# Merge weights of a head pair right behind its last scores: moving the merge of dilated attention forward by two groups

## The chip, the cores and the metric

The kernel runs on one core of one Trainium2 chip. The metric is the device time of one execution in microseconds. The engines are called PE (matmuls; PEld are its weight loads), DVE, ACT, POOL and SP as in the profile. The instructions of each stand in one queue in a fixed order; DMAs are issued from such queues too, here from SP and POOL.

## The reference

One layer of a decoder: RMSNorm, one projection, two mixers side by side, output projection, a conv FFN. The change touches mixer A for the prompt of 2048 positions, softmax attention of 8 heads of 64 elements over three patterns:

```python
PATTERNS = ((128, 1), (512, 4), (2048, 16))      # window, dilation

def combine_patterns(results):
    outs = jnp.stack([o for o, _ in results], axis=0)
    lses = jnp.stack([l for _, l in results], axis=0)
    w = jax.nn.softmax(lses, axis=0)
    return jnp.sum(w[..., None] * outs, axis=0)

def prompt_attn(q, k, v):
    return combine_patterns([dilated_prompt(q, k, v, w, d) for w, d in PATTERNS])
```

Each pattern gives an output and the logarithm of its softmax denominator; the three outputs are merged per head and position with weights from the three denominators.

## The kernel before

The program has three stages: the projections with the linear-attention mixer and the sample tokens (`sweeps`), the prompt's dilated attention (`attention`), and the output projection and FFN (`tail`). A planner sets the order of instructions on each engine: it goes by the order in which they are written, by its own estimate of when each is ready, and by order edges (`after`) that the program adds by hand.

`attention` goes through 4 pairs of heads (`pr`), in each through 3 patterns (`pat`), in each through 4 groups of query blocks (`g`): 12 groups to a pair. A group is one unit (pattern 2) or two (patterns 0 and 1). A unit (`AtUnit`) has three steps. `qk_` does its scores on PE (L1817), their masking and row minimum on DVE (L1822), and the exponentials with their row sums on ACT (L1826); minima and sums go to the statistics tile `aml` of the pair and pattern. `t` transposes the exponentials on PE (L1843) and copies them out of PSUM (L61 on ACT or L63 on DVE). `pv` multiplies by the values (L1860), and the last unit of a group copies the result (L63) into `OP[pat]`, the tile `aop`. Units wait in a list, `fifo`: `drain(3)` lets up to three units be behind in their `pv`. PE's unit steps are chained by hand in the order written.

Patterns 1 and 2 read their queries in an order that needs a gather: POOL copies them into `aqg` (`at_gather`, L1125, two copies to a group), called from `qk_` two groups ahead, in the groups 2 to 9 of each pair, for the groups 4 to 11.

`at_merge` merges the three outputs of one pair. It is a generator: each `next` issues one step. For the pairs 0 to 2:

- step 1, the weights: 8 selecting matmuls bring the statistics of patterns 0 and 2 into one order (`pam`, L1134 and L1137), then a chain of small DVE instructions (L1143 to L1175) with one exponential on ACT (L1166), a transpose on PE (L1189) and a copy to `awt` (L63);
- step 2: POOL stores `awt` to memory (`d_awd`, L1194);
- step 3: POOL issues the loads that bring the weights of the first block of columns back, each spread over 64 partitions (`awb`, L1182);
- then two steps for each of four blocks of columns: (a) the loads of the next block, two products and an addition (L1224, L1224, L1209), and (b) a product, an addition into `amo` and the store to `mixa` (L1224, L1234, L1236), all on POOL.

`line` chains all of these POOL instructions and the gathers in the order in which they are written, so POOL's queue is the program's order. At the end of every group `attention` issues one step of the merge that is under way. Before the change a merge was created when the pair's last unit left `fifo`, which is in the second group of the next pair; so step 1 stood at the end of group 1 of the next pair, the store at the end of group 2, the first loads at the end of group 3, and the blocks in groups 4 to 11. The `aop` pool has 5 tiles, `awb` 2, `amo` 2, `aqg` 5.

The last pair (`pr` 3) does without memory: POOL does the small steps of its weights, POOL and ACT spread them (L1219, L1217), PE transposes them (`pab`, L1221) and DVE multiplies (L1222). All of it is written behind the last unit's values.

Of the kernel before, what the change touches and what calls it, by code (L numbers as in the profile page):

```python
# [36 lines left out]
class Layer:  # L37
# [944 lines left out]
    def attention(self):  # L982
        with ExitStack() as ctx:
            self.aq[1] = self.pool(ctx, "at1")
            p = self.ap = self.pool(ctx, "at")
            self.app = self.pool(ctx, "atp", bass.MemoryType.PSUM)
            self.ev = 0
            pend = None
            fifo = []
            sk = self.AB["skew"]  # L990

            def drain(n):
                nonlocal pend
                if len(fifo) > sk[0]:
                    fifo[-1 - sk[0]].t()
                while len(fifo) > n:
                    un = fifo.pop(0)
                    un.t()
                    un.pv()
                    if un.last:  # L1000
                        for _ in pend or ():
                            pass
                        pend = self.at_merge(un.pr, un.ML, un.OP)

            if self.AB['man']:
                eng = mybir.EngineType
                ctx.enter_context(self.tc.manual_schedule(engines={getattr(eng, e) for e in self.AB['man']}))
            self.vq = []
            self.at_loadv(0)
            self.at_loadv(1)  # L1010
            for _ in self.at_load(0, ((1, 2),), to=self.qk0):
                pass
            rest = self.at_load(0, ((2, 4),), to=self.qk0)
            self.qgn = []
            for _ in range(self.AB["qg"]):
                p.tile([128, 4, 128], F32R, name=self.n("aqg"), tag="aqg", bufs=self.AB["qg"])
            for pat in range(3):
                for _ in range(2):
                    p.tile([128, 16, 4], F32, name=self.n("aml"), tag=f"aml{pat}", bufs=2)
            for _ in range(2):  # L1020
                p.tile([128, 3, 4, 128], F32, name=self.n("awb"), tag="awb", bufs=2)
            for _ in range(2):
                p.tile([128, 512], F32, name=self.n("amo"), tag="amo", bufs=2)
            pre = iter(())
            for pr in range(4):
                if pr == 3:
                    self.rctx.close()
                    pre = self.wo_pre()
                qk = self.qk0
                nxt = self.at_load(pr + 1) if pr < 3 else iter(())  # L1030
                ML, OP = [], []
                for pat in range(3):
                    base = 16 * (3 * pr + pat)
                    ml = p.tile([128, 16, 4], F32, name=self.n("aml"), tag=f"aml{pat}", bufs=2)
                    op = p.tile([128, 4, 512], F32, name=self.n("aop"), tag="aop", bufs=self.AB["op"])
                    ML.append(ml)
                    OP.append(op)
                    for g in range(4):
                        if base // 4 + g + 2 < 48:
                            self.at_loadv(base // 4 + g + 2)  # L1040
                        for _ in rest:
                            pass
                        po = [None]
                        nu = 1 if pat == 2 else 2
                        for u in range(nu):
                            fifo.append(AtUnit(self, pr, pat, g, u, nu, qk, base, ML, OP, po))
                            fifo[-1].qk_()
                            drain(sk[1])
                            if pat:
                                next(pre, None)  # L1050
                        if pend is not None:
                            next(pend, None)
                        if 5 <= 4 * pat + g < 11:
                            self.qk0 = next(nxt, self.qk0)
            for _ in pre:
                pass
            drain(0)
            for _ in pend:
                pass
# [53 lines left out]
    def line(self, ins):  # L1113

        if self.atpo is not None:
            self.after(ins, self.atpo)
        self.atpo = ins
        return ins
# [10 lines left out]
    def at_merge(self, pr, ML, OP):  # L1129
# [48 lines left out]
        def weights(cb):  # L1178
            W = p.tile([128, 3, 4, 128], F32, name=self.n("awb"), tag="awb", bufs=2)
            if not last:  # L1180
                for h in range(2):
                    line(nc.gpsimd.dma_start(W[64 * h:64 * h + 64],  # L1182
                                           bass.AP(tensor=wd.tensor, offset=wd.offset + 1536 * (2 * cb + h),
                                                   ap=[[0, 64], [512, 3], [128, 4], [1, 128]])))
            return W

        if not last:
            pt = pp.tile([128, 512], F32, name=self.n("pab"), tag="am", bufs=AB["am"])
            nc.tensor.transpose(pt[:96, :128], awf, self.ident)  # L1189
            wt = p.tile([128, 512], F32, name=self.n("awt"), tag="amo", bufs=2)[:96, :128]  # L1190
            self.evac(wt, pt[:96, :128], "v")
            wd = self.a["awd"][pr]
            yield
            line(nc.gpsimd.dma_start(wd, wt))  # L1194
            yield
            nxt = weights(0)
            for _ in range(AB["mw"]):
                yield
        tags = ("am", "ao", "ao")
        j = 0  # L1200
        for cb in range(4):
# [811 lines left out]
```

## Time and profile before

| | |
|---|---|
| time, median of 3 runs | 2808.04 us (2801.09 to 2809.57) |
| profiled execution: time, span, granted clock | 2800.35 us, 2798.5 us, 0.98 |
| PE, DVE, ACT, POOL busy | 2682.2, 1841.5, 1269.1, 593.4 us |
| DMA | 656.82 MB, mean 235 GB/s |
| first and last scores of prompt attention (L1817) | 776.8 and 1073.8 us |

A line of the profile gives the engine, the line of the kernel, the operation, the tile written and those read (numbers left out), and its form. In the order of time it begins with the start and the busy time in us and may end with the idle time of that engine ahead of it and what ended it, in brackets. A line of waits gives the waiting engine, tile and line, what it waited for, the sum in us, the number of waits and the longest. A line of stretches gives each engine's busy time with the number of its instructions, the granted clock of TensorE (1.00 is full speed), the share of DMA and GB/s.

### The profile page before, as it was taken

The numbers are of one execution on the slowest core, as the hardware profiler recorded it, in microseconds if no ns is written. First come the engines' busy times: TensorE is split into PE (matmuls) and PEld (weight loads), VectorE is DVE, ScalarE is ACT, GpSimd is POOL, SyncE is SP. The second block draws the span as 40 slices with busy tenths as digits, with TensorE's granted clock in tenths as the row PEclk, the third lists the DMA queues.
The fourth block names the chain that finished last, engine by engine and source line by source line (L and its number), as shares of the span: only waits on it lengthen the run. The fifth ranks groups of instructions, "written<-read, shape, count | busy, mean of one in ns | idle before, by whom it ended". The sixth has DMA issues, their size and how long they took to land. (4 is left out here: it accounts for less than half of the span.)

```text
span 2798.5 us, 58530 instructions
## 1 busy us (share of the span) xinstructions
PE 2682.2 (96%) x22203; PEld 2538.9 (91%) x22203; DVE 1841.5 (66%) x4578; ACT 1269.1 (45%) x2959; POOL 593.4 (21%) x741
## 2 busy tenths in 40 slices
PE   7999999999989998998999998999999999999997
PEld 6889899788778887998899998999999999999997
DVE  7667655444357777466999888676577766666666
ACT  6535433333257776344554444434244333343332
POOL 3424242443333666013000011000020000200001
PEclk9999999999999999998999999999999999999998
DMA  8755446789798764367578677886698875976654
GB/s 302 258 177 181 168 129 208 269 329 361 269 211 174 185 165 141 102 231 254 195 275 297 224 273 291 290 297 223 211 333 282 298 237 198 328 255 215 219 186 147
DMA packets 283594, 656.82 MB, mean 235 GB/s; under 512 B 31841, under 2 KB 81633, under 8 KB 281265
## 3 DMA queue, kind: packets, MB, share of 16 engines
q1 hardware_dynamic: 253008, 574.66, 61.1%
q0 software_dynamic: 13216, 46.56, 5.1%
q10 hardware_dynamic: 17088, 31.86, 3.1%
q8 instruction: 175, 2.87, 0.4%
q14 instruction: 107, 0.87, 0.1%
HBM read 509.02 MB, written 143.94 MB: 233 GB/s over the span
## 5 line engine op out<-in xcount | busy, mean ns | idle before, releaser
L68 ACT ACTIVATE ws<-wr 128x512 fp32r<-128x512 f32 (+1 forms) x482 | 292.9, 616 | 432.4 <-PE pfe L1585 139.1
L90 PE MATMUL pfd<-hh,ws 128*128 128x264 f32 x2816 | 476.9, 286 | 8.3 <-ACT ws L68 6.7
L90 PEld LDWEIGHTS pfd<-hh,ws 128*128 128x128 f32 x2816 | 401.4, 189 | 11.2 <-ACT ws L68 8.6
L71 DVE TENSOR_TENSOR ws<-wr,ws 128x512 fp32r<-128x512 f32 (+1 forms) x482 | 320.0, 670 | 135.8 <-ACT ws L68 131.0
L90 PE MATMUL pfd<-hl,ws 128*128 128x264 f32 x1408 | 303.7, 285 | 0.0
L1585 PE MATMUL pfa<-xh,ws 128*128 128x264 f32 x1496 | 292.8, 287 | 6.8 <-ACT ws L68 2.4
L1585 PE MATMUL pfe<-xh,ws 128*128 128x264 f32 x1496 | 288.6, 285 | 4.2 <-DVE u L1572 2.9
L1585 PE MATMUL pfd<-xh,ws 128*128 128x264 f32 x1408 | 288.0, 285 | 2.8 <-DVE up L1572 2.4
L1585 PEld LDWEIGHTS pfa<-xh,ws 128*128 128x128 f32 x1496 | 237.3, 190 | 8.7 <-ACT p L1574 2.9
L1585 PEld LDWEIGHTS pfe<-xh,ws 128*128 128x128 f32 x1496 | 235.9, 189 | 4.9 <-DVE u L1572 3.3
L398 PE MATMUL pv<-wh,xh 128*128 128x256 f32 (+1 forms) x816 | 234.1, 287 | 1.1 <-DVE th L695 1.1
L1585 PEld LDWEIGHTS pfd<-xh,ws 128*128 128x128 f32 x1408 | 230.7, 189 | 3.8 <-DVE up L1572 3.0
L398 PE MATMUL pv<-wl,xh 128*128 128x256 f32 (+1 forms) x816 | 232.0, 284 | 0.0
L398 PE MATMUL pv<-wh,xl 128*128 128x256 f32 (+1 forms) x816 | 231.9, 284 | 0.0
L90 PEld LDWEIGHTS pfd<-hl,ws 128*128 128x128 f32 x1408 | 226.8, 189 | 0.1
L1534 POOL DMA_DIRECT2D xl<-d_xst x52 | 28.6, 550 | 894.5 <-PE pfe L1585 866.0
L1826 ACT ACTIVATE ass<-ass,aml 128x256 f32<-128x256 f32 (+1 forms) x384 | 173.6, 454 | 89.8 <-DVE aml L1822 88.6
L1585 PE MATMUL pfd<-xl,ws 128*128 128x264 f32 x704 | 200.2, 285 | 0.0
L90 PE MATMUL pq<-xh,wh 128*128 128x512 f32 (+2 forms) x480 | 175.4, 373 | 10.2 <-ACT xh L236 7.7
L1613 DVE TENSOR_TENSOR acc<-acc,pfd 128x264 f32<-128x264 f32 x304 | 116.7, 424 | 91.0 <-PE pfd L90 90.9
L1585 PE MATMUL pfe<-xl,ws 128*128 128x264 f32 x616 | 175.4, 285 | 0.0
L1585 PE MATMUL pfa<-xl,ws 128*128 128x264 f32 x616 | 175.2, 284 | 0.0
(341 smaller groups left out, 6691.4 us busy)
## 6 DMA issues: line engine op xcount, KB each, us to landing
ws<-d_wst SPq DMA_DIRECT2D x248, 512.0 KB
wr<-in_wu SPq DMA_DIRECT2D x114, 512.0 KB
d_wst<-ws SPq DMA_DIRECT2D x88, 512.0 KB
wr<-in_wd SPq DMA_DIRECT2D x160, 256.0 KB
wr<-in_wt SPq DMA_DIRECT2D x60, 512.0 KB
wh<-d_wbs SPq DMA_DIRECT2D x35, 512.0 KB
wl<-d_wbs SPq DMA_DIRECT2D x35, 512.0 KB
skp<-in_ckt SPq DMA_DIRECT2D x16, 1024.0 KB
```

What stands on the lines that cost most here:

```text
L68: h = nc.scalar.activation(hi, src, AF.Copy)
L71: return h, (nc.gpsimd if lo_eng == "p" else nc.vector).tensor_tensor(lo, src, hi.bitcast(F32), op=ALU.subtract)
L90: mm = nc.tensor.matmul(o, ww[:, k, :], xx[:, s0:s0 + n], start=(k == order[0] and i == 0), stop=(k == order[-1] and i == 2))
L398: mm = nc.tensor.matmul(ps[:m, :256], x[:, t0:t0 + m], w[:, k % 4, :], start=(k == 0 and i == 0), stop=(k == KT - 1 and i == 2))
L1534: self.nc.gpsimd.dma_start(t.bitcast(F32), xo[i, z])
L1585: self.lastmm = nc.tensor.matmul(bank[:, :H], w[:, ww, k, :], xx, start=new and k == 0 and j == 0, stop=k == 3 and j == 2, skip_group_chec ...
L1613: nc.vector.tensor_tensor(acc[m][:, s0:s0 + n], acc[m][:, s0:s0 + n], pz, op=ALU.add)
L1826: ex = nc.scalar.activation(ssb[:, sc:sc + nk], ssb[:, sc:sc + nk], AF.Exp, bias=self.ml[:, idx, h:h + 1], scale=-1.0, accum_out=self.ml[: ...
```

## The change

A merge is created in the group that issues the pair's last scores, as soon as the last unit is in `fifo`, and its first step is issued at the end of that group (group 11 of the pair itself). All steps of the pairs 0 to 2 so stand two groups further ahead: the store at the end of group 0 of the next pair, the first loads at the end of group 1, the blocks in groups 2 to 9. For the last pair a `yield` splits the generator behind the weights: the weights are written in group 11, ahead of the last units' transposes and values, and the rest behind them as before. The generators take 12 steps as before.

```diff
@@ attention, in drain() @@
                     un = fifo.pop(0)
                     un.t()
                     un.pv()
-                    if un.last:
-                        for _ in pend or ():
-                            pass
-                        pend = self.at_merge(un.pr, un.ML, un.OP)
@@ attention, in the loop over groups @@
                             drain(sk[1])
                             if pat:
                                 next(pre, None)
+                        if fifo[-1].last:
+                            for _ in pend or ():
+                                pass
+                            pend = self.at_merge(pr, ML, OP)
                         if pend is not None:
                             next(pend, None)
@@ at_merge @@
             nxt = weights(0)
             for _ in range(AB["mw"]):
                 yield
+        else:
+            yield
         tags = ("am", "ao", "ao")
```

## The prediction

> **What bounds the kernel now.** I read the page first, then the busy time by stretches of the attention stage, then its waits, then the order of time on POOL, PE and DVE around the three merges that are moved.
>
> ```profile
> span 2798.5 us, 58530 instructions
> PE 2682.2 (96%) x22203; PEld 2538.9 (91%) x22203; DVE 1841.5 (66%) x4578; ACT 1269.1 (45%) x2959; POOL 593.4 (21%) x741
> 860.00:880.00 20.00, 19.97 (x209) 17.31 (x208) 17.88 (x81) 17.92 (x65) 2.74 (x3) 1.00 0.99 190
> 920.00:940.00 20.00, 17.22 (x154) 15.63 (x156) 11.89 (x46) 11.67 (x48) 16.86 (x16) 0.83 0.94 212
> 980.00:1000.00 20.00, 14.69 (x130) 12.89 (x127) 8.41 (x53) 12.91 (x58) 19.45 (x21) 0.88 0.65 167
> PE pas L1817 <- POOL aqg L1125: 17.1, 9, 4.0
> POOL aop L1224 <- DMA awb<-d_awd: 17.8, 3, 9.4
> ```
>
> PE is busy for 96% of the span, so the kernel as a whole is TensorE's. The three stretches (columns after the length: PE, PEld, DVE, ACT, POOL, granted clock, DMA share, GB/s) show that a pair of prompt attention has two halves. From 860 to 880 PE is full and POOL nearly idle; from 920 to 940 and from 980 to 1000 POOL is at 17 to 19 of 20 us, PE drops to 17.2 and 14.7, and its clock to 0.83 and 0.88. The two waits say why: PE's scores wait for the gathered queries (aqg) that POOL writes, and POOL's merge products (L1224) wait for the weights that come back from memory (awb). POOL is one queue in a fixed order, so a gather stands behind every merge step written ahead of it. Here it is for head pair 1 (the second):
>
> ```profile
> 844.91 1.15 POOL L1125 CAST aqg<-aqs 128x512 fp32r<-128x512 f32 x1 [1.47 <-issue]
> 873.79 0.53 POOL L1194 DMA_DIRECT2D d_awd<-awt  x1 [27.73 <-PE pao L1860]
> 874.31 2.22 POOL L1125 CAST aqg<-aqs 128x512 fp32r<-128x512 f32 x2
> 880.38 1.05 POOL L1182 DMA_DIRECT2D awb<-d_awd  x2 [3.85 <-DMA d_awd<-awt]
> 881.42 2.23 POOL L1125 CAST aqg<-aqs 128x512 fp32r<-128x512 f32 x2
> 883.57 1.02 POOL L1182 DMA_DIRECT2D awb<-d_awd  x2
> 894.01 2.49 POOL L1224 TENSOR_TENSOR aop<-aop,awb 128x512 f32<-128x512 f32 x2 [9.42 <-DMA awb<-d_awd]
> 897.79 2.11 POOL L1125 CAST aqg<-aqs 128x512 fp32r<-128x512 f32 x2
> 922.70 2.02 POOL L1125 CAST aqg<-aqs 128x512 fp32r<-128x512 f32 x2
> 924.68 1.27 POOL L1224 TENSOR_TENSOR aop<-aop,awb 128x512 f32<-128x512 f32 x1
> 928.24 2.50 POOL L1224 TENSOR_TENSOR aop<-aop,awb 128x512 f32<-128x512 f32 x2
> 932.04 1.28 POOL L1224 TENSOR_TENSOR aop<-aop,awb 128x512 f32<-128x512 f32 x1
> ```
>
> I call the eight gathers of a pair G0 to G7 (G7 feeds its last group of scores) and the halves of the four merge blocks 0a, 0b to 3a, 3b. G0 is done at 846. The merge's store (L1194) sits idle for 27.7 us until its weights are there, G1 follows, the first broadcast loads (L1182) wait 3.85 us for the store, G2 follows, and 0a starts only at 894.01. From there POOL runs without a gap: 0a, G3 (897.79), 0b, G4, 1a, G5, 1b, G6, 2a, G7 (922.70), and then, with no gather left in this pair, 2b (924.68), 3a (928.24) and 3b (932.04).
>
> **The chain that sets a pair's length.** Four rows of each pair give it: the first scores (T), the weights' copy (awt), the first product (0a), and the last group's scores as PE takes them up behind G7.
>
> ```profile
> 851.39 0.33 PE L1817 MATMUL pas<-akh,aqs 128*128 128x128 f32 x1
> 873.22 0.28 DVE L63 COPY awt<-pab 96x128 f32<-96x128 f32 x1
> 923.78 0.48 PE L1817 MATMUL pas<-akh,aqg 128*128 128x128 f32 x1 [2.78 <-POOL aqg L1125]
> 930.76 0.33 PE L1817 MATMUL pas<-akh,aqs 128*128 128x128 f32 x1
> 953.40 0.28 DVE L63 COPY awt<-pab 96x128 f32<-96x128 f32 x1
> 968.79 2.52 POOL L1224 TENSOR_TENSOR aop<-aop,awb 128x512 f32<-128x512 f32 x2 [6.19 <-DMA awb<-d_awd]
> 998.75 0.47 PE L1817 MATMUL pas<-akh,aqg 128*128 128x128 f32 x1 [2.78 <-POOL aqg L1125]
> 1005.79 0.33 PE L1817 MATMUL pas<-akh,aqs 128*128 128x128 f32 x1
> 1027.62 0.28 DVE L63 COPY awt<-pab 96x128 f32<-96x128 f32 x1
> 1039.21 2.98 POOL L1224 TENSOR_TENSOR aop<-aop,awb 128x512 f32<-128x512 f32 x2 [2.14 <-DMA awb<-d_awd]
> 1070.54 0.48 PE L1817 MATMUL pas<-akh,aqg 128*128 128x128 f32 x1 [2.80 <-POOL aqg L1125]
> ```
>
> Pair 1: T to awt 21.8 us, awt to 0a 20.8, 0a to last scores 29.8, last scores to the next T 7.0: together 79.4. Pair 2: 22.6 + 15.4 + 30.0 + 7.0 = 75.0. Pair 3: 21.8 + 11.6 + 31.3. In all three PE waits 2.8 us for POOL at the last group, so this chain, not PE's own work, sets the length.
>
> **The change, part by part.**
>
> *POOL's order.* Every merge step moves ahead by two groups in a queue whose order is the program's; gathers keep theirs. New order of a pair: store, W0 loads, G0, 0a, G1, 0b, G2, 1a, G3, 1b, G4, 2a, G5, 2b, G6, 3a, G7, 3b. So between 0a's start and G7 there now also lie 2b (924.68 to 928.24: 3.56 us), 3a (928.24 to 932.04: 3.80) and two more gathers, G1 and G2 (2.02 each as at 922.70): 11.4 us more on the third leg, in each of three pairs. Before, G1 and G2 ran inside the wait for the loads, for nothing, and 2b, 3a, 3b ran while PE did the next pair's first groups, which need no gather. Both covers go. G0, done at 846 before, now stands behind the W0 loads; with the times below it ends 29 us after T. That is a new stall, but it and those at G1 to G6 lie on the same POOL chain and are not added. The second loads (L1182, 1.02) stay inside the landing wait. 3a and 3b, and so the mixa store, come out before the next merge; nothing waits for them sooner.
>
> *The weights.* Their share is the first leg. The first step is written two groups sooner, but the planner had already put it ahead of its place:
>
> ```profile
> 851.50 0.39 ACT L1826 ACTIVATE ass<-ass,aml 128x128 f32<-128x128 f32 x1
> 855.46 1.00 PE L1137 MATMUL pam<-aml,atab 128*128 128x64 f32 x8
> 856.86 0.42 DVE L1143 TENSOR_TENSOR atm<-pam,atab 128x256 f32<-128x256 f32 x1
> 937.83 0.42 DVE L1143 TENSOR_TENSOR atm<-pam,atab 128x256 f32<-128x256 f32 x1
> 1011.88 0.40 DVE L1143 TENSOR_TENSOR atm<-pam,atab 128x256 f32<-128x256 f32 x1
> ```
>
> The last exponential of pair 0 starts at 851.50, so the softmax statistics are complete 0.5 us after T; the selecting matmuls start at 855.46, and DVE's first merge step 5.5, 7.1 and 6.1 us after T. From there to awt it takes 16.4, 15.6 and 15.7 us, because DVE does scores and copies between the small dependent steps. Written sooner, the first step can start at about T + 2.5 (0.5, a matmul slot of about 0.6, 1.4 from pam to DVE as now). For the rest I take 14.5 us, a little under today's 16: in the second half of today's chain the merge already stands ahead of the work that is let in, and other work slips in all the same. So awt comes at T + 17.0, sooner by 4.8, 5.6 and 4.8: 15.2 us. Bounds: nothing at all (planner as now), and, from the last merge, whose chain runs nearly alone:
>
> ```profile
> 1077.75 1.10 PE L1137 MATMUL pam<-aml,atab 128*128 128x64 f32 x8
> 1080.77 1.99 DVE L63 COPY aop<-pao 128x512 f32<-128x512 f32 x2
> 1085.31 1.09 PE L1860 MATMUL pao<-apt,av 128*64 128x128 f32 x14 [0.16 <-DVE apt L63]
> 1086.79 2.37 POOL L1219 TENSOR_SCALAR awb<-aaw 128x512 f32<-128x512 f32 x4
> 1088.38 0.69 DVE L1222 TENSOR_TENSOR aop<-aop,pab 128x512 f32<-128x512 f32 x1 [0.86 <-PE pab L1221]
> ```
>
> 9.0 us from pam to the finished weights, plus some 1.5 for the transpose and copy, from T + 1.1: awt at T + 11.6 at best, 10.2 sooner in pair 1. That is still under the 11.4 that the third leg grows by.
>
> *Second leg.* Store and loads move with awt; I keep 20.8, 15.4 and 11.6. The loads' landing is most of it, and it is longest where DMA is full (share 0.99 in 860 to 880). Six microseconds sooner is still inside that stretch, so neither gain nor loss; bounds are the 11.6 of pair 3 for all (13.0 less in total), or 3 us more in each of the first two.
>
> The Trainium skill (DMA: Bandwidth & Descriptors, "Anatomy of one DMA — SWDGE (gpsimd) path") puts a GpSimd DMA at 2.0 us plus its bytes over 436 KB/us, which is 2.9 us for these 384 KB. By that the second leg would be an estimated 7 us, 27 us would go, and the time would fall to about 2798. The trace disagrees: POOL waits 9.42 us for the landing at 894.01, with both loads long issued. No term here uses it.
>
> *The last pair.* Its weights no longer follow the last values. pam can move from 1077.75 to behind the last exponential (about 1.2 us sooner), the two copies inside its chain (1.99 us at 1080.77) drop behind it, and POOL is free earlier, since only 3b follows G7. Finished weights would come 3 us sooner than 1086.79, but PE has the last values until 1086.4 (1085.31 + 1.09) and DVE then starts a full row of products at 1088.38. I take 2 us gained, between 0 and 3.5. The added yield costs nothing: it only splits the generator.
>
> *Sum.* 3 x 11.4 = 34.2, less 15.2, less 2: 17 us slower, all of it on PE's path, since PE has no slack before or after the stage. Against the profiled execution (2800.35 us, span 2798.5) this gives 2817; the median of the runs shown is 7.7 us above that execution, so I forecast 2825.
>
> **Rivals.**
> 1. *The planner leaves the weights where they are* (the change does not do what it says). For it: pam already runs far ahead of its written place. Against it: the 5 to 7 us between T and DVE's first step are order, not data. Then nothing pays for the 11.4: 32 to 34 us slower, 2841.
> 2. *Break-even.* The small steps, now ahead of all scores in the planner's list, close up to some 10 us; 9 to 10 of the 11.4 come back in each pair, and the tail pays the rest. 2800 to 2816, middle 2810. For it, the 9.0 us above; against it, the second half of today's chains.
> 3. *Faster: the broadcast loads land sooner.* One place, the wait at 0a: if loads issued at T + 24 instead of T + 29 met a thinner DMA load and all pairs took pair 3's 11.6, that is 13.0 us; with weights at T + 11.6 (31 us sooner) the sum is 34.2 - 31.4 - 13.0 - 2, that is 12 us faster, 2796. It decides only when weights and landing together gain more than 13.5 us a pair ((34.2 - 2 + 8.4) / 3). For it, only pair 3; against it, the full DMA stretch.
>
> **How the numbers follow.** 0.3%, 8.4 us here, is about what a measurement can tell from no change. Chances: my forecast, with 6 to 23 us back from the weights (9 to 26 slower), 0.65; rival 1, 0.14; rival 2, 0.13; rival 3, 0.08. Range 2806 to 2838: it leaves out rival 3, the better half of rival 2 and the far part of rival 1. Slower 0.79, same 0.13, faster 0.08. My likeliest case alone is 2817 to 2834.
>
> **What would show it.** Right: L1143 some 2.5 us behind T; awt near T + 17; G1 behind 0a, so that PE waits for aqg already in the dilation-4 groups (about 10 us at the sixth group of pair 1), and PE's waits for aqg grow from 17.1 to over 40 us; 0a to last scores 41 us; pairs of 86 and 81 us, and 71 from T to the last scores of pair 3 (64.7 now). Wrong: a pair shorter than today's; gathers ahead of the merge in POOL's order; awt before T + 11; a second leg under 11 us.

## The result and the profile after

| | before | after |
|---|---|---|
| median of 4 runs, us | 2804.89 (2801.09 to 2809.57) | 2835.05 (2829.06 to 2840.35) |
| ratio | | 1.0119, 95% interval 1.0100 to 1.0138 |
| profiled execution: span, granted clock | 2798.5 us, 0.980 | 2830.8 us, 0.974 |

The change makes the kernel 30 us slower by the medians (33 us by the ratio). First the two lines of the page that say how much PE did:

```profile
span 2830.8 us, 58520 instructions
...
PE 2694.0 (95%) x22203; PEld 2547.4 (90%) x22203; DVE 1843.5 (65%) x4578; ACT 1269.7 (45%) x2959; POOL 591.7 (21%) x741
```

PE does the same 22203 matmuls, but is busy for 11.8 us longer (2682.2 before), and idle for 20.5 us longer (span less busy: 136.8 against 116.3). Both come almost wholly from the attention stage, from its first scores to 1085 us (before) and 1117.5 us (after): PE is busy there for 276.7 and 287.3 us, idle for 31.5 and 51.4. Busy time by stretches, same columns as before the change:

```profile
860.00:880.00 20.00, 18.27 (x191) 15.87 (x187) 17.42 (x77) 16.36 (x59) 1.86 (x4) 1.00 1.01 198
920.00:940.00 20.00, 18.08 (x136) 16.21 (x135) 9.62 (x60) 12.78 (x57) 14.08 (x14) 0.74 0.62 153
980.00:1000.00 20.00, 15.50 (x136) 13.71 (x138) 9.88 (x46) 10.89 (x42) 19.38 (x19) 0.83 0.42 117
```

From 920 to 940 PE is busy for 18.08 us with 136 matmuls; before it was busy for 17.22 us with 154. It does less and looks busier: the granted clock fell to 0.74 (0.83 before). The waits of the stage, here and below counted from 845 us on, that is from the second pair on, name the same two waits as before:

```profile
POOL d_awd L1194 <- DVE awt L63: 78.4, 3, 31.6
...
PE pas L1819 <- POOL aqg L1125: 27.2, 14, 6.4
POOL aop L1226 <- DMA awb<-d_awd: 17.4, 3, 7.6
POOL awb L1182 <- DMA d_awd<-awt: 12.9, 3, 7.6
PE pam L1134 <- ACT ass L1828: 4.8, 3, 1.6
```

PE waits for gathered queries 14 times instead of 9, for 27.2 us instead of 17.1. The last line is new: three times, PE's queue stands at a selecting matmul until ACT has done an exponential. POOL's own order of time in pair 1, and the first products of pairs 2 and 3, show why:

```profile
875.68 0.53 POOL L1194 DMA_DIRECT2D d_awd<-awt  x1 [31.60 <-DVE awt L63]
878.66 1.05 POOL L1182 DMA_DIRECT2D awb<-d_awd  x2 [2.45 <-DMA d_awd<-awt]
879.70 2.13 POOL L1125 CAST aqg<-aqs 128x512 fp32r<-128x512 f32 x2
881.77 1.02 POOL L1182 DMA_DIRECT2D awb<-d_awd  x2
889.03 2.48 POOL L1226 TENSOR_TENSOR aop<-aop,awb 128x512 f32<-128x512 f32 x2 [6.24 <-DMA awb<-d_awd]
...
892.79 2.12 POOL L1125 CAST aqg<-aqs 128x512 fp32r<-128x512 f32 x2
...
929.39 2.04 POOL L1125 CAST aqg<-aqs 128x512 fp32r<-128x512 f32 x2
931.39 1.27 POOL L1226 TENSOR_TENSOR aop<-aop,awb 128x512 f32<-128x512 f32 x1
...
979.61 2.48 POOL L1226 TENSOR_TENSOR aop<-aop,awb 128x512 f32<-128x512 f32 x2 [7.56 <-DMA awb<-d_awd]
...
1058.51 2.51 POOL L1226 TENSOR_TENSOR aop<-aop,awb 128x512 f32<-128x512 f32 x2 [3.61 <-DMA awb<-d_awd]
```

Only G0 (879.70) now runs inside the wait for the loads. G1 (892.79) stands behind the product 0a, and G7 (929.39) stands behind everything but 3b (931.39). The other rows of the chain, first from PE (first scores T of a pair, last group's scores), then from DVE (first merge step L1143, weights' copy awt):

```profile
853.11 0.33 PE L1819 MATMUL pas<-akh,aqs 128*128 128x128 f32 x1
...
930.48 0.33 PE L1819 MATMUL pas<-akh,aqg 128*128 128x128 f32 x1 [1.75 <-POOL aqg L1125]
...
937.48 0.37 PE L1819 MATMUL pas<-akh,aqs 128*128 128x128 f32 x1
...
1021.06 0.33 PE L1819 MATMUL pas<-akh,aqg 128*128 128x128 f32 x1 [0.79 <-POOL aqg L1125]
...
1025.03 0.33 PE L1819 MATMUL pas<-akh,aqs 128*128 128x128 f32 x1
...
1102.26 0.33 PE L1819 MATMUL pas<-akh,aqg 128*128 128x128 f32 x1 [0.19 <-POOL aqg L1125]
```

```profile
857.91 0.42 DVE L1143 TENSOR_TENSOR atm<-pam,atab 128x256 f32<-128x256 f32 x1
...
875.11 0.28 DVE L63 COPY awt<-pab 96x128 f32<-96x128 f32 x1
...
941.44 0.42 DVE L1143 TENSOR_TENSOR atm<-pam,atab 128x256 f32<-128x256 f32 x1 [1.65 <-PE pam L1137]
...
959.24 0.28 DVE L63 COPY awt<-pab 96x128 f32<-96x128 f32 x1
...
1028.95 0.42 DVE L1143 TENSOR_TENSOR atm<-pam,atab 128x256 f32<-128x256 f32 x1 [1.59 <-PE pam L1137]
...
1046.80 0.28 DVE L63 COPY awt<-pab 96x128 f32<-96x128 f32 x1
```

The four legs in us, from these rows and those of before:

| leg | before, pairs 1 / 2 / 3 | after | forecast of the difference, sum | measured, sum |
|---|---|---|---|---|
| T to awt | 21.8 / 22.6 / 21.8 | 22.0 / 21.8 / 21.8 | -15.2 | -0.8 |
| awt to 0a | 20.8 / 15.4 / 11.6 | 13.9 / 20.4 / 11.7 | 0 | -1.8 |
| 0a to last scores | 29.8 / 30.0 / 31.3 | 41.4 / 41.5 / 43.8 | +34.2 | +35.6 |
| last scores to next T | 7.0 / 7.0 / - | 7.0 / 4.0 / - | 0 | -3.0 |
| pair | 79.4 / 75.0 / 64.7 | 84.4 / 87.6 / 77.2 | +19 | +30.0 |

The pairs explain 30.0 of the 32.3 us between the two spans; 2.0 more stand already at the first scores of the stage (778.86 against 776.91), ahead of all that was changed. The fourth leg of pair 2 is 3.0 us shorter as its matmuls ran at up to twice the rate: the last group's scores start 0.11 us apart there and 0.21 us apart in the kernel before (rows in the last section).

### The profile page after: what moved, and what is told of

It is laid out like the page before. It is cut to its first block, busy times and chain, and to the rows that moved or that the text cites. A ratio compares the mean times of both kernels' runs of the same rounds, so it can differ in the third digit from the quotient of the medians.

```text
span 2830.8 us, 58520 instructions
## 1 busy us (share of the span) xinstructions
PE 2694.0 (95%) x22203; PEld 2547.4 (90%) x22203; DVE 1843.5 (65%) x4578; ACT 1269.7 (45%) x2959; POOL 591.7 (21%) x741
## 5 line engine op out<-in xcount | busy, mean ns | idle before, releaser
L90 PEld LDWEIGHTS pfd<-hh,ws 128*128 128x128 f32 x2816 | 402.5, 190 | 11.4 <-ACT ws L68 7.9
L1824 DVE CUSTOM_DVE_ANT_0 ass<-pas,atab 128x256 f32<-128x256 f32 (+1 forms) x384 | 118.9, 362 | 95.4 <-PE pas L1819 84.4
L1615 DVE TENSOR_TENSOR acc<-acc,pfd 128x264 f32<-128x264 f32 x304 | 116.4, 423 | 91.1 <-PE pfd L90 90.7
```

The lines of the kernel that those rows point to most:

```text
L90: mm = nc.tensor.matmul(o, ww[:, k, :], xx[:, s0:s0 + n], start=(k == order[0] and i == 0), stop=(k == order[-1] and i == 2))
L1615: nc.vector.tensor_tensor(acc[m][:, s0:s0 + n], acc[m][:, s0:s0 + n], pz, op=ALU.add)
L1824: red = nc.vector.tensor_tensor_reduce(ssb[:, sc:sc + nk], ps[:, sc:sc + nk], L.amk[self.pat][:, 256 - nk:256], scale=1.0, scalar=3e38, op ...
```

## The experiments

The theory after the result: POOL's order costs its 11.4 us a pair in full, and the weights came no sooner, since DVE mixes scores and copies into the merge's chain of small instructions. The rivals were: it is the loads' landing in a DMA-full stretch that decides; something in the last pair; or PE is simply slower because of its clock. In the table the legs are sums over the pairs 1 to 3 of one profiled execution (fourth leg left out), so they scatter by a few us against the medians. e6, e7 and e9 are given in the text alone. "Before" is the kernel before in the same series of runs.

| kernel | T to awt | awt to 0a | 0a to last scores | time, us | before, us | ratio (95%) |
|---|---|---|---|---|---|---|
| before | 66.3 | 47.8 | 91.1 | | | |
| after | 65.5 | 46.0 | 126.7 | 2835.05 | 2804.89 | 1.0119 (1.0100 to 1.0138) |
| e1 | 67.3 | 49.2 | 97.7 | 2800.54 | 2800.14 | 1.0006 (0.9989 to 1.0022) |
| e2 | 65.5 | 44.9 | 118.4 | 2810.23 | 2800.14 | 1.0032 (1.0017 to 1.0048) |
| e3 | 63.0 | 62.3 | 86.7 | 2802.70 | 2800.14 | 1.0004 (0.9990 to 1.0019) |
| e4 | 48.3 | 53.3 | 129.3 | 2819.73 | 2800.14 | 1.0064 (1.0043 to 1.0085) |
| e5 | 56.8 | 54.0 | 95.8 | 2799.34 | 2800.24 | 1.0000 (0.9985 to 1.0015) |
| e8 | 103.8 | 34.6 | 91.4 | 2823.42 | 2800.24 | 1.0088 (1.0066 to 1.0110) |
| e10 | 69.0 | 51.5 | 91.7 | 2801.37 | 2799.32 | 1.0006 (0.9991 to 1.0021) |
| e11 | 55.4 | 54.3 | 93.7 | 2794.66 | 2799.32 | 0.9982 (0.9970 to 0.9994) |
| e12 | 54.6 | 50.9 | 126.6 | 2827.31 | 2799.32 | 1.0100 (1.0075 to 1.0125) |
| e13 | 38.4 | 45.8 | 128.8 | 2805.72 | 2801.70 | 1.0019 (1.0002 to 1.0035) |
| e14 | 46.4 | 71.7 | 93.4 | 2803.78 | 2801.70 | 1.0012 (0.9997 to 1.0027) |

**e1: the change, with the products back in their old groups.** Store and first loads stay early; POOL's products stand where they stood before.

```diff
-    AB = dict(mw=1, ...
+    AB = dict(mw=3, ...
```

> Weights, store and first loads stay at their new places, but the products wait two more groups, so that POOL's order from 0a on is that of before (0a, G3, 0b, G4 ... 2a, G7, 2b, 3a, 3b). Theory (the loss is the two merge halves and two gathers that the change put ahead of G7, 11.4 us a pair, and the weights come no sooner): third leg back to 30 us, time as before, 2805 within 8 us. Rival (the loss lies in the earlier weights or in how the planner lays out the rest): stays at 2835.

The third leg falls back from 126.7 to 97.7 us and the time to that of before: with weights as late as they are, the order of products and gathers on POOL is the whole loss. PE's longer busy time goes with it: 2680.1 us for the same 22203 matmuls, against 2694.0 in the change, so the lower clock is a consequence of the order and no cause of its own. PE's waits for gathers nearly vanish, and others take their place. Waits in the stage of e1:

```profile
PE pao L1862 <- DMA av<-out_o_vp: 14.6, 3, 6.0
...
PE pas L1819 <- POOL aqg L1125: 4.7, 2, 2.8
```

PE now waits 14.6 us for the value tiles (av) that SP loads. That is the wait that stands behind the gathers.

**e2 and e3: one group at a time.** e2 is the change with the products one group later than the change has them; e3 is the kernel before with the products one group later still. The edit is the same in both.

```diff
-    AB = dict(mw=1, ...
+    AB = dict(mw=2, ...
```

> As the change, but the products wait one more group: one half (2b, 3.6 us) and one gather (2.0) ahead of G7 more than before, not two of each. Theory: third leg 35.5 us, 5.6 us a pair over before, 17 us in all, about 2822, half way. Rival (a threshold: PE absorbs one group): 2805 or 2835.

> The kernel before, with the products one group later: G3 goes ahead of 0a, and 2a (4.8 us) and a gather leave the stretch ahead of G7. Theory: third leg 6.8 us shorter in each of three pairs, up to 20 us faster, 2785, if PE's own work of some 65 us a pair allows. Rival: pattern 2's output tile must wait for 3a (five aop tiles), the stall moves behind the last scores and the time stays at 2805 or rises.

e2 lies between (third leg 118.4), nearer to before in time than half way. e3 was a miss: I had expected a gain from a third leg that gets shorter. It did get shorter, by 4.4 us in all, but the second grew by 14.5, since a later product is a later 0a. PE's new waits are again those for values and, with five output tiles, for a free one. None of the three other places of the products beats that of before; e3's cannot be told from it in time.

**e4: the change, with the small steps on POOL.** Eleven of the small instructions of the weights of pairs 0 to 2 go from DVE to POOL, where nothing stands between them; the reductions, the minima and the reciprocal stay on DVE.

```diff
-        em, line = (nc.gpsimd, lambda x: x) if pr == 3 else (nc.vector, self.line)
+        em, line = nc.gpsimd, ((lambda x: x) if pr == 3 else self.line)
```

> The change, with the eleven small steps of the weights (L1164, L1169, L1170, L1171, L1175) on POOL, which is idle then, for every pair. Theory (awt is late because DVE puts scores and copies between the small dependent steps): awt at about T + 17 instead of T + 22, 4 to 5 us a pair, about 2821. Rival (the chain is as long by itself, or POOL's slower steps make up for it): 2835 or more.

The first leg falls by 17 us, to 17.7, 18.5 and 12.2 us, which is what the prediction had counted on (T + 17.0), and the time to 2819.73: 19.6 us above the kernel before (ratio 1.0064), where the prediction's sum was 17. So the sum holds in total when its weights term is supplied. Leg by leg it does not: against before the four legs come to -18.0, +5.5, +38.2 and -6.3 us.

**e5: the kernel before, with the same edit.** The diff is that of e4.

> The kernel before, with the eleven small steps of the weights on POOL for every pair. Theory (POOL's chain sets the pairs, so whatever brings awt forward by 4 to 9 us comes back in the time until the next thing is late): up to 12 us faster than before, 2790. Rival (behind the chain the value loads (av) are late next, as in the runs where the products waited longer): no gain, 2800 within 5.

Weights 9.5 us sooner bring nothing there: 1.0000. PE's waits for gathers go down to 2.2 us, and those for values go up to 13.1 us.

**e6 and e7: free weights.** In e6 (the change) and e7 (the kernel before), the weights of the pairs 0 to 2 are not computed: a constant third replaces the selecting matmuls, the small steps and the exponential. Transpose, store, loads and products stay.

```diff
+        if pr < 3:
+            aw = p.tile([128, 96], F32, name=self.n("aaw"), tag="aaw", bufs=2)
+            nc.vector.memset(aw, 1.0 / 3.0)
+        else:
...
```

> The change, with a constant third in place of the computed weights for pairs 0 to 2: the selecting matmuls, the small steps and their exponential are left out, so that the store waits for nothing; transposes, store, loads and products stay. Theory (the change needs weights that come early, and they do not): the first leg of a pair is gone, 0a starts some 20 us after T and POOL is done with G7 at about T + 62, near PE's own 62 to 66; some 45 us faster than the change, 2790, unless value loads are late next (then 2800). Rival (the order itself costs PE 11 us a pair whatever the weights do): 2825 or more.

> The kernel before with the same constant weights for pairs 0 to 2. Theory: 0a starts at about T + 29, when G2 has its buffer, G7 comes at T + 60, PE's own work is the bound: 2785 to 2800, the same as the change with constant weights within 8 us, so the order costs only where the weights are late. Rival (the order costs by itself): 11 to 30 us faster than the change with constant weights.

e6 took 2789.54 us, ratio 0.9965 (0.9950 to 0.9980) to the kernel before; e7 took 2797.92 us, 0.9997 (0.9986 to 1.0008). In e6 awt is written ahead of the pair's first scores in all three pairs. With weights that cost nothing, the changed order is the faster one, and the list of waits has none of PE's for gathers. In the order of before, free weights are worth nothing. The next wait in e6 is the values' again:

```profile
PE pao L1868 <- DMA av<-out_o_vp: 15.8, 7, 9.2
```

Of the versions of the change that were run, this one alone is faster than before; with weights 12 to 13 us after T (e13 below) it is not. Where between the two it begins to pay was not measured.

**e8: the kernel before, SP's loads in their written order.** Each load of queries, keys and values of this stage on SP waits, by an order edge, for the one written ahead of it. It tests whether the second leg is set by other loads.

```diff
+    def spline(self, on, ins):
+        if on:
+            if self.atsp is not None:
+                self.after(ins, self.atsp)
+            self.atsp = ins
...
-                e.dma_start(t[:, j, :], ...)
+                self.spline(i > 1, e.dma_start(t[:, j, :], ...))
```

> The kernel before, with SP's loads of keys, queries and values for attention chained in the order in which the program writes them: the next pair's 6 MB no longer start at T, but 32 us later, and the value loads do not stand behind them. Theory (the second leg is long because the broadcast loads share full DMA queues with that burst): awt to 0a falls to about 11.6 us in pairs 1 and 2, 13 us faster, 2787. Rival: the keys then come late for the next pair, PE waits for them at T, and the time stays or rises.

The second leg becomes 11.8, 11.5 and 11.3 us, the same in all three pairs. POOL's rows of pair 1 in e8, and the stretch they lie in:

```profile
883.24 1.05 POOL L1190 DMA_DIRECT2D awb<-d_awd  x2
...
891.71 2.52 POOL L1232 TENSOR_TENSOR aop<-aop,awb 128x512 f32<-128x512 f32 x2 [2.33 <-DMA awb<-d_awd]
```

```profile
860.00:880.00 20.00, 20.00 (x201) 17.64 (x199) 18.64 (x79) 14.34 (x53) 0.00 (x0) 0.95 0.17 48
880.00:892.00 12.00, 12.00 (x126) 10.72 (x122) 8.34 (x38) 9.38 (x36) 7.29 (x10) 1.00 0.70 150
```

From first loads to 0a it takes 8.5 us (883.24 to 891.71) where before took 13.6 (880.38 to 894.01), with DMA at a share of 0.17 ahead of it instead of 0.99. The store takes 1.8 us from issue to landing where it took 6.3, and the first two loads 6.3 us where they took 12.0 (medians). The landing is slow where SP's burst of loads runs. The edit is no gain, because other loads now come late: PE waits 20.7 us for the keys (akl, akh) and 9.3 us for values.

**e9: the last pair alone.** The kernel before, with only the last pair's merge made at the new place. The diff is against the change, whose split of the generator stays.

```diff
+                    if un.last and un.pr < 3:
+                        for _ in pend or ():
+                            pass
+                        pend = self.at_merge(un.pr, un.ML, un.OP)
...
-                        if fifo[-1].last:
+                        if fifo[-1].last and pr == 3:
```

> The kernel before, with the weights of the last pair alone written behind its last scores; the merges of pairs 0 to 2 stay where they were. The prediction's term for this part was 2 us gained (0 to 3.5). Theory now (PE and DVE order there hardly moves, 27.9 us from the last group's scores to the output projection against 27.8): no difference, within 4 us of before. Rival: 2 to 4 us faster.

2798.76 us against 2799.32: 1.0000 (0.9985 to 1.0016). From the last group's scores to the second row of the output projection it takes 27.4 us, 27.8 in the kernel before, 27.9 in the change. The last pair is worth nothing either way.

**e10, e11 and e12: the burst of loads moved.** SP's loads in written order as in e8, and the next pair's keys written from group 1 on instead of group 5. e10 is the kernel before with this, e11 adds the small steps on POOL, e12 is the change with both.

```diff
-                        if 5 <= 4 * pat + g < 11:
+                        if 1 <= 4 * pat + g < 7:
```

> The kernel before, with SP's attention loads chained in written order and the next pair's keys and queries written in groups 1 to 6 instead of 5 to 10, so that they start some 10 us behind T, between the value loads. Theory (with all of them 32 us later the second leg fell to 11.5 us but the keys were late): keys are in time, awt to 0a comes down to between 11.6 and 20.8, value loads are not late: 5 to 12 us faster, 2792. Rival (burst and broadcast loads still meet): 2800 within 4.

> As the run with keys from group 1, and the small steps of the weights on POOL as well. With POOL's chain 4 us shorter a pair and the value loads ahead of the burst, both things that were late give way: pairs of 70 us, 12 to 18 us faster than before, 2785. Rival (a third thing is late, or the planner's new order eats it): 2795 to 2800.

> The change with both of these. Theory: its third leg of 41 to 43 us stays, so it remains slower than the same two edits on the kernel before by 5 to 11 us a pair: 2805 to 2815. Rival (with earlier weights and thinner DMA queues the new order pays): at or under 2790.

e10 gains nothing: the burst is moved, the second leg is as long as before (21.0, 19.3, 11.2). e11 is the only kernel with the full computation that was measured faster than before, 0.9982 (0.9970 to 0.9994); I had expected more. Its first leg is 10.9 us shorter, its second and third give 9.1 back. e12 is slower than I had expected: its third leg, 126.6 us, is that of the change, and neither edit touches it. Its three legs add up to 232 us, those of e4 to 231, so the moved loads brought nothing; what is left of the difference between the two times stays open.

**e13: the change, with its chain left alone on DVE.** One order edge holds back the score reductions (L1822 before) of the next pair's second unit until the merge's last small step is done.

```diff
+            self.mlast = em.tensor_tensor(at(i), at(i), rc(mm), op=ALU.mult)
...
+                if h == 0 and blk == info[0][0] and (self.pr > 0, self.pat, self.g, self.u) == (True, 0, 0, 1):
+                    L.after(red, L.mlast)
```

> The change, with one order edge a pair: DVE's first row minimum of the second unit of the next pair stands behind the last small step of the weights, so that scores no longer come between these steps. Theory (awt comes no sooner in the change because the planner lets DVE's other work in between the small steps): awt at T + 11 to 13 instead of T + 22, some 9 us off each of three pairs, 2835 down to about 2808, though PE now waits for scores' buffers at the pair's start. Rival (the chain is that long by its own dependences, or PE's wait gives it all back): 2830 or more.

This one is a hit. The weights come 13.4, 13.3 and 11.6 us after T, 27 us sooner in all, and the time falls to 2805.72 us, 4 us above the kernel before (ratio 1.0019). DVE's rows of pair 1 in the change, then in e13 (lines there are two further on: L1145 is L1143):

```profile
868.82 0.19 DVE L1170 TENSOR_TENSOR amm<-adn 128x32 f32<-128x32 f32 x1
868.92 0.42 DVE L1824 CUSTOM_DVE_ANT_0 ass<-pas,atab 128x256 f32<-128x256 f32 x1
...
869.27 0.69 DVE L63 COPY apt<-pat 128x512 f32<-128x512 f32 x1
869.87 0.19 DVE L1171 TENSOR_TENSOR amm<-amm,adn 128x32 f32<-128x32 f32 x1
869.97 0.69 DVE L63 COPY aop<-pao 128x512 f32<-128x512 f32 x1
870.57 0.35 DVE L1173 RECIPROCAL amm<-amm 128x32 f32<-128x32 f32 x1
```

```profile
861.82 0.42 DVE L1145 TENSOR_TENSOR atm<-pam,atab 128x256 f32<-128x256 f32 x1 [0.55 <-PE pam L1139]
...
867.20 0.19 DVE L1172 TENSOR_TENSOR amm<-adn 128x32 f32<-128x32 f32 x1
867.43 0.19 DVE L1173 TENSOR_TENSOR amm<-amm,adn 128x32 f32<-128x32 f32 x1
867.65 0.35 DVE L1175 RECIPROCAL amm<-amm 128x32 f32<-128x32 f32 x1
...
870.45 0.28 DVE L63 COPY awt<-pab 96x128 f32<-96x128 f32 x1
```

In the change a score reduction and two copies stand between three small steps (L1170, L1171, L1173); from the first step (857.91) to awt (875.11) it takes 17.2 us. In e13 the same steps follow one another, and it takes 8.6. That settles where the weights' time went.

**e14: all edits at once.** e1's order, e13's edge, SP's loads in written order, keys from group 1.

> Everything that helped at once: weights written behind the last scores with the same edge, store and first loads at their new places, products two groups later as before, keys from group 1 with SP's loads in written order. Theory: neither POOL's chain nor late values hold a pair, 2780 to 2790. Rival (PE's wait for the chain at each pair's start, some 5 us, eats it, or keys meet the broadcast loads): 2795 to 2805.

A miss: 1.0012 (0.9997 to 1.0027). The first leg is 20 us shorter than before, the second 24 longer. POOL's rows of pair 1 show what 0a stood behind:

```profile
874.80 1.05 POOL L1190 DMA_DIRECT2D awb<-d_awd  x2 [6.01 <-DMA d_awd<-awt]
875.84 5.51 POOL L1133 CAST aqg<-aqs 128x512 fp32r<-128x512 f32 x5
889.94 1.13 POOL L1133 CAST aqg<-aqs 128x512 fp32r<-128x512 f32 x1 [8.59 <-PE pas L1827]
891.02 1.02 POOL L1190 DMA_DIRECT2D awb<-d_awd  x2
892.05 2.53 POOL L1234 TENSOR_TENSOR aop<-aop,awb 128x512 f32<-128x512 f32 x2
```

Not the loads: 0a has no wait of its own. The sixth gather copy ahead of it waits 8.59 us for PE's scores; five copies ran just before it, and aqg has five tiles, so I read it as waiting for PE to give one back. By that reading 0a cannot start in the order of before until PE has taken up the first gathered queries of the pair, however early the weights are. e7 agrees: its first loads were issued at 851.29, and yet 0a started only at 882.71, behind a gather copy that had waited for PE:

```profile
880.62 1.13 POOL L1125 CAST aqg<-aqs 128x512 fp32r<-128x512 f32 x1 [27.17 <-PE pas L1823]
```

More aqg tiles would test it; that was not tried.

## Why the prediction was right and wrong

The direction held, the size did not: 30 us measured, 17 forecast. That the time still lies in the range is luck as far as the forecast's own case goes: that case alone ended at 2834, and only the share of rival 1 took the range to 2838.

- **POOL's order** (third leg, 3 x 11.4 us) was right: 11.7, 11.5 and 12.4 us, and e1 gives them back when the products alone move back. New order, G0's end 28.7 us after T, and uncovered G1 and G2 were as written.
- **The weights** are the step that failed: "The weights. Their share is the first leg", 15.2 us expected, 0.8 measured. The first step should have come to about T + 2.5; it came 4.8, 4.0 and 3.9 us after T, sooner against T than before by 0.7, 3.1 and 2.2. And the rest, which I took as 14.5 us, grew to 17.2, 17.8 and 17.9 (16.4, 15.6 and 15.7 before). I had read the mixing in the trace of before and still took the chain as getting shorter by being written ahead of the scores. It was written ahead, and scores and copies slipped in all the same; e13 shows the remedy was an order edge, not a place in the program. e4 shows the rest of the sum standing in total: with weights at 17.7, 18.5 and 12.2 us after T the loss is 19.6 us. e13 does too: weights 27.1 us sooner leave 34.2 less 27.1, that is 7 us, less the 2 for the last pair, and 4 were measured.
- **Rival 1** gave 2841 for weights that stay where they are. In its effect, it is what happened (2835); its wording, that the planner leaves the first step in place, is not quite: the step moved, the end of the chain did not.
- **Second leg**: kept in sum (-1.8 us), not pair by pair: 13.9 and 20.4 us in pairs 1 and 2 where 20.8 and 15.4 had stood. e8 shows its size following other loads, as the prediction had it. The estimate from the Trainium skill (DMA: Bandwidth & Descriptors, "Anatomy of one DMA — SWDGE (gpsimd) path"), some 7 us for this leg, was met nowhere: the shortest on record is 9.7, in pair 3 of e2.
- **The last pair**: 2 us expected, nothing found, alone (e9) as in the change.
- **Signs**: I had expected PE's waits for aqg to pass 40 us; they reached 27.2. The pairs grew by 30 us all the same: of the 32.3 us of the span, 10.1 are these waits, 11.8 are PE's longer busy time, and 10.4 are other idle time of PE. The selecting matmuls' waits for an exponential, which the prediction had at nothing, are 4.8 us of that, though no run shows whether they cost time; the rest stays open. The wait at pair 1's sixth group was 6.4 us at the most, not 10.

The third rival, faster by loads that land sooner, did not come about, though e6 shows its side of the ledger: with free weights the new order is 0.9965 of before.

## What to carry to other kernels

Moving steps forward in a queue shared with another stream has a price that can be read off: the work that now stands ahead of the other stream's last item (here 11.4 us a pair, to within 1). The gain, on the other hand, is only there if what the moved steps wait for comes sooner too; writing a chain of small instructions earlier does not make it finish earlier while a planner may fill the gaps between them. Before shortening one wait, look up which comes next: here the value loads (13 to 16 us of PE's waits in e1, e5 and e6) and, by the reading of e14, the five query tiles stood right behind it.

## What the hardware showed that I had not expected

- Fewer matmuls, more busy time: from 920 to 940, 136 matmuls in 18.08 us of busy time at a granted clock of 0.74, against 154 in 17.22 at 0.83. Over the whole execution PE was busy 11.8 us longer for the same 22203 matmuls. PE's rows show where: behind the wait of 2.78 us ahead of the last group's scores (before, 923.78) the matmuls start 0.21 us apart, behind one of 0.79 us (after, 1021.06) 0.11 us apart. The next two of each:

```profile
924.06 0.42 PE L1817 MATMUL pas<-akl,aqg 128*128 128x128 f32 x1
924.27 0.41 PE L1817 MATMUL pas<-akh,aqg 128*128 128x128 f32 x1
...
1021.22 0.28 PE L1819 MATMUL pas<-akl,aqg 128*128 128x128 f32 x1
1021.33 0.27 PE L1819 MATMUL pas<-akh,aqg 128*128 128x128 f32 x1
```

In both traces, from the second pair on, each of the eight waits for gathered queries of 2.4 us and more has matmuls 0.21 us apart behind it. After three shorter ones (1.68 to 1.75 us) they went over to 0.21 us within the next group, after others (1.49 and 2.21 us) not, so the length of the wait does not decide alone. A PE that waits often in this stage so loses more than its waits. No edit tested this by itself.

- The second leg went with DMA's share in it. In the kernel before it took 20.8, 15.4 and 11.6 us at shares of 0.93, 0.77 and 0.55; in e8 11.8, 11.5 and 11.3 us at 0.69, 0.64 and 0.56. The share does not tell all: in pair 1 of the change it took 13.9 us at 0.94.
